# A hybrid decoder layer on one core: low parts of the first weights dealt by hand, and the 64-to-128 step of a block inverse in fours in one PSUM bank

## The chip, the cores and the metric

The kernel runs on one core of a Trainium2 chip. The metric is device time in microseconds of one execution: 1597.19 us before, the median of three runs (1596.48 to 1598.59).

## The reference

One layer over 256 positions of width 2048, in float32. From the vector c come a shift, a scale and a gate (adaLN). Then, in the reference's own words:

```
h = RMSNorm_pre(x) * (1 + scale) + shift
[gdn_qkv | gdn_a | gdn_b | gdn_z | ml_qk | ml_v | ml_i | ml_f | ml_o | ml_z | g_A | g_B] = h W_in
y_A = W_pA( RMSNorm_head(GatedDeltaNet(conv(q, k, v), decay, beta)) * silu(gdn_z) )
y_B = W_pB( sigmoid(ml_o) * RMSNorm_head(mLSTM(conv(q, k), v, i, f)) * silu(ml_z) )
out = (sigmoid(g_A) * y_A + sigmoid(g_B) * y_B) W_out
x <- x + gate * RMSNorm_post(out)
```

The gated delta rule has 32 value heads of 128 on 16 key heads. In it a triangular system `unit_lower @ sol = rhs` is solved per head. The kernel solves it over blocks of 128 positions, so each head needs the inverse of two unit triangular 128 x 128 matrices.

## The kernel before

**The stream.** All large products take 2048-wide weights from memory in units of 1 MB (`load_w`, three buffers). A unit is used in two pieces of 1024 columns. For float32 accuracy each piece is split into a high part `whi` (a rounding copy on ACT, line 169) and a low part `wlo` (a subtraction, line 170, on DVE or on POOL), four buffers each; each product is three matmuls, high x high, high x low and low x high (`mm3`, line 227). `Stream.run` writes the order out: it prepares pieces until more than `ahead` are waiting (1 in the first units, then 3), uses one, calls `after`, and then calls `side.step()`. The kernel is in program order on each engine; no scheduler reorders it.

**The side work.** `Side.step()` advances every generator by one `yield`, lower rank first. So "a step" is one piece of the stream on PE with what the generators issue behind it. Each of PE's small works takes PSUM banks from a ring of four (`gtile`, `banks`, `gfree`): `banks(n)` yields until the next n banks of the ring have been given back in an earlier step. `side.debt` is a reckoning of DVE's load that only decides in which step the base inverse (`base_inverse`) issues its next DVE instructions.

**The beginning.** `first_chunk` (popped from `begin`) is the preparation of the first unit: it issues `keep_busy` matmuls on zeros, the squares of x, the adaLN sums of chunk 0, and chunk 0 of h. x is transposed on PE two chunks at a time (`x_turn`, evicted by ACT, line 338). An adaLN unit `ar` (1 MB, three buffers) is one DVE instruction (line 414) that gives one sum; `h_chunk(k)` needs the two sums of chunk k and makes chunk k of h: `sh`, `s1`, `hf`, then its high and low part. For chunk 1 DVE makes `sh` and `s1` (lines 417 to 420), for the later ones ACT (lines 388 and 389). `BLOCKS` (in `add_start_groups`) say which of the first 14 column groups use which chunks of h, and when the next adaLN unit is put between. Partial sums go to `part` (lines 473, 475, 477).

Which engine makes a low part in this stretch is said by `split_w`: `share[0]` starts at -320 and gains 0.8 of the width at each call; once it is at least the width, POOL takes the piece. When the last adaLN unit is prepared the share becomes 0 and DVE takes all.

**The delta rule.** It runs in eight groups zg of four heads. A period of the stream has 24 pieces: 8 of a q, k, v, v projection (PSUM tile `pt`), 8 of a z projection (`pn`), and 8 of the next `pt`. Each `pt` starts a `gdn_stage1`: convolution (four ACT products at line 651, then DVE at 657), the score matmuls `psa`, `psb` and the transposes `psv` after `yield from banks(3)`, then in the following steps the DVE products that make `au`, and last the right hand sides `rr` (ACT, line 762), four steps behind `psa`. `rr` has two buffers, one group in each.

`base_inverse` makes the inverses of the 32-blocks on DVE. `gdn_stage2` then joins them on PE and applies them: 32-blocks to 64-blocks in two steps (`mp` line 846, `mx` lines 857 and 860), 64-blocks to 128 in two steps (`mq` line 872, evicted to `p2` on ACT, then `mz` line 881, evicted to `x0` on ACT), and then `pa` (893), `pb` (901), `pc` (911) and `po` (919 to 922) with waits of one or two steps between; ACT's line 912 evicts `pc` into `ys`, which line 922 reads. It has rank 0, the first stages rank 1, `base_inverse` rank 2.

Of the kernel before, what the change touches and what calls it, by code (L numbers as in the profile page):

```python
# [9 lines left out]
AF = mybir.ActivationFunctionType  # L10
ALU = mybir.AluOpType
# [4 lines left out]
P = 128  # L16
S = 256
D = 2048
KC = D // P
# [5 lines left out]
START_SHARE = 0.8  # L25
# [92 lines left out]
def hybrid_layer_kernel(  # L118
# [25 lines left out]
    V, A, T, G, SP = nc.vector, nc.scalar, nc.tensor, nc.gpsimd, nc.sync  # L144
# [23 lines left out]
    def split(src, hi, lo, eng=None):  # L168
        A.copy(hi, src)  # L169
        (eng or V).tensor_tensor(lo, src, hi.bitcast(F32), op=ALU.subtract)  # L170

    share = [-320.0, START_SHARE]
    begin = []

    def split_w(src, hi, lo):

        n = src.shape[1]
        share[0] += share[1] * n
        if share[0] >= n:
            share[0] -= n  # L180
            split(src, hi, lo, G)
        else:
            split(src, hi, lo)
# [14 lines left out]
    def gtile(nm, held=False):  # L198
        i = slots[0] % 4
        slots[0] += 1  # L200
        t = pg.tile([P, 512], F32, name=nm, tag="g")
        freed[i] = 1 << 30 if held else side.t + 1
        slots[1][id(t)] = i, t
        return t

    def gfree(t):
        freed[slots[1].pop(id(t))[0]] = side.t

    def banks(n):

        while any(freed[(slots[0] + j) % 4] >= side.t for j in range(n)):
            yield
# [16 lines left out]
    side = Side()  # L229
# [35 lines left out]
    ad = sp.tile([P, 32], F32, name="ad")  # L265
    s1 = sp.tile([P, KC], F32, name="s1")
    sh = sp.tile([P, KC], F32, name="sh")
# [20 lines left out]
    bat = cp.tile([P, 32], F32, name="bat")  # L288
    npre = cp.tile([P, KC], F32, name="npre")
# [8 lines left out]
    zero = part[-1][:, 0]  # L298
    G.memset(zero, 0.0)
    zps = jtile("zps")  # L300

    def keep_busy(n):

        for _ in range(n):
            T.matmul(zps, zero[:, 0:P], zero, start=True, stop=True)

    late_c = {}

# [33 lines left out]
    bnp = sp.tile([P, KC], F32, name="bnp")  # L342
# [6 lines left out]
    def first_chunk(src, hi, lo):  # L349


        keep_busy(4)
        half = [slice(i * 1024, (i + 1) * 1024) for i in range(2)]
        for b in range(2):
            for i in range(2):
                if b == 0 and i == 1:
                    V.scalar_tensor_tensor(part[3].rearrange("p b c -> p (b c)"), xs[:, b, half[i]], 1.0,
                                           xs[:, b, half[i]], op0=ALU.mult, op1=ALU.mult, accum_out=ss[:, b, i:i + 1])
                else:
                    A.activation(part[2].rearrange("p b c -> p (b c)"), xs[:, b, half[i]], AF.Square,  # L360
                                 accum_out=ss[:, b, i:i + 1])
        G.tensor_tensor(rs, ss[:, :, 0], ss[:, :, 1], op=ALU.add)
        G.tensor_scalar(rs, rs, 1.0 / D, EPS, op0=ALU.mult, op1=ALU.add)
        pow_(rs, rs, mhalf[:, 0:2])
        for k in (0, 2, 4, 6, 8):
            x_scale(k)
        ada_sum(ar0, slice(0, D), ad[:, 0:1])
        V.scalar_tensor_tensor(bnp, bat[:, KC:2 * KC], 1.0, npre, op0=ALU.add, op1=ALU.mult)
        for i in range(2):
            ada_sum(ar1, half[i], adh[:, i:i + 1])  # L370
        V.tensor_tensor(ad[:, KC:KC + 1], adh[:, 0:1], adh[:, 1:2], op=ALU.add)
        V.scalar_tensor_tensor(s1[:, 0:1], ad[:, KC:KC + 1], npre[:, 0:1], bnp[:, 0:1], op0=ALU.mult, op1=ALU.add)
        A.activation(sh[:, 0:1], ad[:, 0:1], AF.Identity, bias=bat[:, 0:1])
        V.tensor_copy(hi, src)
        xps = x_turn(0)
        keep_busy(1)
        V.tensor_tensor(lo, src, hi.bitcast(F32), op=ALU.subtract)
        hf = sp.tile([P, S], F32, name="hf", tag="hf", bufs=2)
        A.activation(hf.rearrange("p (b t) -> p b t", b=2), xps[:, :, 0], AF.Identity, bias=sh[:, 0:1],
                     scale=s1[:, 0:1])  # L380
        split(hf, h_hi[:, 0], h_lo[:, 0], V)
        A.copy(xs[:, :, P:2 * P], xps[:, :, 1])
    begin.append(first_chunk)

    def h_chunk(k):

        if k > 1:
            A.activation(sh[:, k:k + 1], ad[:, k:k + 1], AF.Identity, bias=bat[:, k:k + 1])
            A.activation(s1[:, k:k + 1], ad[:, KC + k:KC + k + 1], AF.Identity, bias=bnp[:, k:k + 1],
                         scale=npre[:, k:k + 1])  # L390
        hf = sp.tile([P, S], F32, name="hf", tag="hf", bufs=2)
        A.activation(hf.rearrange("p (b t) -> p b t", b=2), xs[:, :, k * P:(k + 1) * P], AF.Identity, bias=sh[:, k:k + 1], scale=s1[:, k:k + 1])
        split(hf, h_hi[:, k], h_lo[:, k], V if k in (1, KC - 1) else G)
# [14 lines left out]
    def ada_units():  # L408

        adders = []  # L410
        for k in range(1, KC):
            for pt in range(2):
                def prep(h, raw, k=k, pt=pt):
                    V.scalar_tensor_tensor(raw, raw, 1.0, csil, op0=ALU.mult, op1=ALU.mult,
                                           accum_out=ad[:, pt * KC + k:pt * KC + k + 1])
                    if k == 1 and pt:
                        V.scalar_tensor_tensor(s1[:, k:k + 1], ad[:, KC + k:KC + k + 1], npre[:, k:k + 1],
                                               bnp[:, k:k + 1], op0=ALU.mult, op1=ALU.add)
                    elif k == 1:
                        V.tensor_tensor(sh[:, k:k + 1], ad[:, k:k + 1], bat[:, k:k + 1], op=ALU.add)  # L420
                    j = 2 * (2 * k + pt) - 4
                    if 4 <= j < 16:
                        x_turn(j)
                        if 6 <= j < 12:
                            x_scale(j + 4)
                    h_chunks(k - 1)
                    if pt == 1:
                        due.append(k)
                        if k == KC - 1:
                            banks_open()  # L430
                    return ()
                adders.append(lambda i=2 * k + pt, prep=prep:
                              stream.add(w_ada[i], prep, None, 1, load=(load_ada, "ada", ADA_BUFS)))
        return adders
# [22 lines left out]
    def add_start_groups(bi):  # L457
# [41 lines left out]
        for g in groups[::per]:  # L499
            st_ = {}  # L500

            def use_piece(h, hi, lo, g=g, st_=st_):
                for i in range(min(2, per * nk - 2 * h)):
                    gg, c = g + (2 * h + i) // nk, (2 * h + i) % nk
                    if c == 0:
                        st_["ps"] = [jtile(f"pn{i}") for i in range(2)]
                    use(gg, st_["ps"], c, hi, lo, i * 512)
                    if c == nk - 1:
                        after(gg, st_["ps"])
                    if bi == 0 and gg == NE - 2:  # L510
                        h_chunks(1)
                    if bi == 0 and gg == 3:
                        x_turn(2)
                stream.ahead = 3 if bi else 1
            src = tuple(w_in[START[g + i]][:, k0 * 512:(k0 + nk) * 512] for i in range(per))
            adders.append(lambda src=src, use_piece=use_piece:
                          stream.add(src, lambda h, raw: prep_w(h, raw, per * nk * 512), use_piece,
                                     (per * nk + 1) // 2))
# [310 lines left out]
    def gdn_stage2(zg, res, zr):  # L829
# [3 lines left out]
        def um(m):  # L833
            return au[m // 4][:, m % 4 // 2, 256 + 384 * (m % 2):384 + 384 * (m % 2)]
# [28 lines left out]
        for t in range(2):  # L863
            r = 64 * t
            A.activation(x0[r:r + 32, :, r + 32:r + 64], cols32(psx[t])[r:r + 32], AF.Copy, scale=-1.0)
            gfree(psx[t])
        yield
        yield from banks(1)
        psp = gtile("mq", True)
        side.debt -= 1.0  # L870
        for m in range(8):
            T.matmul(psp[64:128, m * 64:(m + 1) * 64], um(m)[0:64, 64:128], y0[:, m], start=True, stop=True)  # L872
        p2 = bp.tile([P, 8, 64], F32, name="p2", tag="p2", bufs=1)
        A.activation(p2[64:128], psp[64:128].rearrange("p (m i) -> p m i", m=8), AF.Copy, scale=-1.0)
        gfree(psp)
        yield
        yield from banks(1)
        psz = gtile("mz", True)
        side.debt -= 1.0
        for m in range(8):  # L880
            T.matmul(psz[0:64, m * 64:(m + 1) * 64], p2[64:128, m], x0[64:128, m, 64:128], start=True, stop=True)  # L881
        A.copy(x0[0:64, :, 64:128], psz[0:64].rearrange("p (m i) -> p m i", m=8))
        gfree(psz)
        yield

        rr = res["rr"].rearrange("p b z (h d) -> p b (z h d)", h=2)
        ys = bp.tile([P, 2, 512], F32, name="ys", tag="ys", bufs=1)
# [587 lines left out]
```

## Time and profile before

| | |
|---|---|
| median of three runs | 1597.19 us |
| profiled execution | 1597.11 us |
| its span | 1595.1 us |
| granted TensorE clock | 0.998 |
| busy share of PE, DVE, ACT, POOL | 99%, 72%, 59%, 16% |

The span is the time between the first and the last instruction of the profiled execution; its own time is 2.0 us longer. PE is the matmul row, and its instructions are pipelined, so a share of 99% says that it hardly ever waits, not that it is at its peak. A row of a timeline gives start, duration, engine, line, operation, output and inputs, and in brackets the idle time ahead of it and what ended it. A row of the chain gives start, duration and what the end of the program was waiting for in that time. A row of the waits gives who waited for whom: total, times, longest.

### The profile page before, as it was taken

The page shows a single profiled execution, that of the slowest core. Times are in us where ns is not written, and L with a number is a line of the kernel's source. Part 1 is how long each engine was busy: PE and PEld are TensorE (multiplying, and loading weights), DVE is VectorE, ACT ScalarE, POOL GpSimd, SP SyncE. Part 2 cuts the span into 40 slices and gives each one's busy share as a digit, 9 for nine tenths or more (in the row PEclk, how much of TensorE's full clock was granted, in tenths as well). Part 3 has the DMA queues.
Part 4 walks back from the last instruction along what each step waited for, and adds up shares of the span by engine and source line. Part 5 has one row for each costly group of instructions (what it writes and reads, how often), then busy time and mean ns, then how long its engine had stood idle before and what let it go on. Part 6 is the DMA issues. An engine that isn't in the chain of part 4 may idle for free.

```text
span 1595.1 us, 25488 instructions
## 1 busy us (share of the span) xinstructions
PE 1581.4 (99%) x9854; PEld 1389.0 (87%) x9854; DVE 1146.5 (72%) x1804; ACT 937.1 (59%) x1494; POOL 250.6 (16%) x206
## 2 busy tenths in 40 slices
PE   8999999999999999999999999999999999999998
PEld 5888888899999999999999999889988878888886
DVE  6776556765689788888878888775768766756654
ACT  7755446765666575757576766665566554444443
POOL 5787761000000010000000000000000000100100
PEclk9999999999999999999999999999999999999999
DMA  9998775965565546555646465546778878766573
GB/s 378 393 387 320 268 295 181 297 234 181 189 190 188 189 156 206 167 182 171 193 159 207 154 195 174 187 165 232 279 268 308 320 275 295 282 248 236 206 274 108
DMA packets 96067, 372.37 MB, mean 233 GB/s; under 512 B 26021, under 2 KB 45877, under 8 KB 58185
## 3 DMA queue, kind: packets, MB, share of 16 engines
q1 hardware_dynamic: 95848, 370.65, 66.4%
q8 instruction: 77, 1.26, 0.3%
q14 instruction: 44, 0.36, 0.1%
q0 software_dynamic: 96, 0.09, 0.0%
q10 hardware_dynamic: 2, 0.01, 0.0%
HBM read 354.40 MB, written 16.31 MB: 232 GB/s over the span
## 4 chain that ended last, share of the span: by engine, by line
PE 84%; issue 12%; DMA 1%; POOL 1%; ACT 0%; DVE 0%; SPq 0%; DVEq 0%; ACTq 0%; POOLq 0%
PE pn L227 37%; PE pt L227 29%; PE py L227 8%; POOL mg L1265 1%; PE psa L227 1%; DMA raw<-in_dram 1%; PE mz L881 1%; PE mq L872 1%; PE csil L297 0%; PE po L922 0%; PE pa L893 0%; PE po L921 0%; PE pc L911 0%; PE po L919 0%; PE pb L901 0%
## 5 line engine op out<-in xcount | busy, mean ns | idle before, releaser
L170 DVE TENSOR_TENSOR wlo<-raw,whi 128x1024 fp32r<-128x1024 f32 x451 | 554.2, 1237 | 264.1 <-ACT whi L169 262.6
L169 ACT CAST whi<-raw 128x1024 fp32r<-128x1024 f32 x516 | 532.2, 1046 | 308.1 <-PE pn L227 154.4
L227 PE MATMUL pt<-h_hi,whi 128*128 128x256 f32 x1280 | 367.8, 287 | 0.0
L227 PE MATMUL pt<-h_hi,wlo 128*128 128x256 f32 x1280 | 362.1, 283 | 0.0
L227 PE MATMUL pt<-h_lo,whi 128*128 128x256 f32 x1280 | 362.0, 283 | 0.0
L227 PE MATMUL pn<-whi,h_hi 128*128 128x512 f32 x896 | 353.0, 394 | 0.3 <-ACT h_hi L169 0.3
L227 PE MATMUL pn<-wlo,h_hi 128*128 128x512 f32 x896 | 349.4, 390 | 1.5 <-POOL wlo L170 1.5
L227 PE MATMUL pn<-whi,h_lo 128*128 128x512 f32 x896 | 349.2, 390 | 0.0
L227 PEld LDWEIGHTS pt<-h_hi,whi 128*128 128x128 f32 x1280 | 245.3, 192 | 1.4
L227 PEld LDWEIGHTS pt<-h_lo,whi 128*128 128x128 f32 x1280 | 245.4, 192 | 0.3
L227 PEld LDWEIGHTS pt<-h_hi,wlo 128*128 128x128 f32 x1280 | 245.2, 192 | 0.0
L227 PEld LDWEIGHTS pn<-wlo,h_hi 128*128 128x128 f32 x896 | 168.4, 188 | 36.6 <-POOL wlo L170 2.7
L227 PEld LDWEIGHTS pn<-whi,h_hi 128*128 128x128 f32 x896 | 168.3, 188 | 35.4 <-ACT h_hi L169 1.1
L227 PEld LDWEIGHTS pn<-whi,h_lo 128*128 128x128 f32 x896 | 168.2, 188 | 35.4
L170 POOL TENSOR_TENSOR wlo<-raw,whi 128x1024 fp32r<-128x1024 f32 (+1 forms) x65 | 150.2, 2321 | 47.8 <-ACT whi L169 47.6
L227 PE MATMUL py<-whi,yhi 128*128 128x512 f32 x384 | 150.7, 392 | 0.0
L227 PE MATMUL py<-whi,ylo 128*128 128x512 f32 x384 | 149.6, 390 | 0.0
L227 PE MATMUL py<-wlo,yhi 128*128 128x512 f32 x384 | 149.5, 389 | 0.0
L473 DVE TENSOR_TENSOR part<-pn,part 128x512 f32<-128x512 f32 x112 | 73.8, 686 | 45.5 <-PE pn L227 45.3
L169 ACT CAST yhi<-ya 128x512 fp32r<-128x512 f32 x48 | 29.9, 622 | 127.8 <-PE py L227 110.9
L657 DVE SCALAR_TENSOR_TENSOR qs<-pt,gcv,qs 128x255 f32<-128x255 f32 (+2 forms) x192 | 92.2, 480 | 4.6
L170 DVE TENSOR_TENSOR ylo<-ya,yhi 128x512 fp32r<-128x512 f32 x48 | 33.2, 691 | 75.4 <-ACT yhi L169 75.4
(269 smaller groups left out, 1810.6 us busy)
## 6 DMA issues: line engine op xcount, KB each, us to landing
raw<-in_dram SPq DMA_DIRECT2D x259, 1024.0 KB
ar<-in_dram SPq DMA_DIRECT2D x31, 1024.0 KB
raw<-in_dram SPq DMA_DIRECT2D x16, 512.0 KB
ya<-o_dr SPq DMA_DIRECT2D x32, 256.0 KB
gate_dr<-part SPq DMA_DIRECT2D x11, 512.0 KB
gb<-rows SPq DMA_DIRECT2D x20, 256.0 KB
raw<-in_dram SPq DMA_DIRECT2D x6, 768.0 KB
ug<-ud SPq DMA_DIRECT2D x32, 128.0 KB
```

The source lines that it names most:

```text
L169: A.copy(hi, src)
L170: (eng or V).tensor_tensor(lo, src, hi.bitcast(F32), op=ALU.subtract)
L227: T.matmul(ps, l, r, start=start and i == 0, stop=stop and i == 2, skip_group_check=True)
L473: V.tensor_tensor(part[g][:, b], ps[b], part[g][:, b], op=ALU.add)
L657: V.scalar_tensor_tensor(dst[:, n, sh:], src[:, 0:S - sh], taps(n, 3 - sh), dst[:, n, sh:], op0=ALU.mult, op1=ALU.add)
L872: T.matmul(psp[64:128, m * 64:(m + 1) * 64], um(m)[0:64, 64:128], y0[:, m], start=True, stop=True)
L881: T.matmul(psz[0:64, m * 64:(m + 1) * 64], p2[64:128, m], x0[64:128, m, 64:128], start=True, stop=True)
L1265: G.tensor_tensor(mcols(b, hf, cg), mcols(b, hf, cg), s_, op=ALU.add)
```

## The change

There are two edits.

*The beginning.* The low parts of the first eight pieces are dealt by a list, `early` (DVE, POOL, POOL, DVE, DVE, POOL, DVE, POOL); behind it the share starts at 0. One of the four `keep_busy` matmuls at the start is 256 columns wide instead of 512. `sh` and `s1` of chunk 1 are made by ACT in `h_chunk`, as for the later chunks. `x_turn(2)` moves from behind the second unit's use to the fourth unit, between the first and the second chunk of its first column group.

*From 64-blocks to 128.* `mq` and `mz` share one bank, `mqz`: `mq` writes partitions 64 to 127, `mz` partitions 0 to 63. The eight matrices go in two fours over three steps: `mq` of the first four; then `mz` of the first four alternating with `mq` of the second four; then `mz` of the second four. Each step evicts its four on ACT. The bank is given back in the third step. The debt is lowered by 0.5 three times instead of by 1.0 twice.

```diff
-    share = [-320.0, START_SHARE]
+    share = [0.0, START_SHARE]
+    early = [V, G, G, V, V, G, V, G]
...
     def split_w(src, hi, lo):
 
         n = src.shape[1]
+        if early:
+            split(src, hi, lo, early.pop(0))
+            return
...
-    def keep_busy(n):
+    def keep_busy(n, cols=512):
 
         for _ in range(n):
-            T.matmul(zps, zero[:, 0:P], zero, start=True, stop=True)
+            T.matmul(zps[:, 0:cols], zero[:, 0:P], zero[:, 0:cols], start=True, stop=True)
...
-        keep_busy(4)
+        keep_busy(3)
+        keep_busy(1, 256)
...
     def h_chunk(k):
 
-        if k > 1:
-            A.activation(sh[:, k:k + 1], ad[:, k:k + 1], AF.Identity, bias=bat[:, k:k + 1])
-            A.activation(s1[:, k:k + 1], ad[:, KC + k:KC + k + 1], AF.Identity, bias=bnp[:, k:k + 1],
-                         scale=npre[:, k:k + 1])
+        A.activation(sh[:, k:k + 1], ad[:, k:k + 1], AF.Identity, bias=bat[:, k:k + 1])
+        A.activation(s1[:, k:k + 1], ad[:, KC + k:KC + k + 1], AF.Identity, bias=bnp[:, k:k + 1],
+                     scale=npre[:, k:k + 1])
...
-                    if k == 1 and pt:
-                        V.scalar_tensor_tensor(s1[:, k:k + 1], ad[:, KC + k:KC + k + 1], npre[:, k:k + 1],
-                                               bnp[:, k:k + 1], op0=ALU.mult, op1=ALU.add)
-                    elif k == 1:
-                        V.tensor_tensor(sh[:, k:k + 1], ad[:, k:k + 1], bat[:, k:k + 1], op=ALU.add)
...
-                    if bi == 0 and gg == 3:
+                    if bi == 1 and gg == NE and c == 0:
                         x_turn(2)
...
         yield from banks(1)
-        psp = gtile("mq", True)
-        side.debt -= 1.0
-        for m in range(8):
-            T.matmul(psp[64:128, m * 64:(m + 1) * 64], um(m)[0:64, 64:128], y0[:, m], start=True, stop=True)
+        psq = psz = gtile("mqz", True)
         p2 = bp.tile([P, 8, 64], F32, name="p2", tag="p2", bufs=1)
-        A.activation(p2[64:128], psp[64:128].rearrange("p (m i) -> p m i", m=8), AF.Copy, scale=-1.0)
-        gfree(psp)
-        yield
-        yield from banks(1)
-        psz = gtile("mz", True)
-        side.debt -= 1.0
-        for m in range(8):
-            T.matmul(psz[0:64, m * 64:(m + 1) * 64], p2[64:128, m], x0[64:128, m, 64:128], start=True, stop=True)
-        A.copy(x0[0:64, :, 64:128], psz[0:64].rearrange("p (m i) -> p m i", m=8))
-        gfree(psz)
-        yield
+        for i in range(3):
+            side.debt -= 0.5
+            first, second = slice(4 * i, 4 * i + 4), slice(4 * i - 4, 4 * i)
+            for m in range(4 * i, 4 * i + 4):
+                if i > 0:
+                    T.matmul(psz[0:64, (m - 4) * 64:(m - 3) * 64], p2[64:128, m - 4], x0[64:128, m - 4, 64:128],
+                             start=True, stop=True)
+                if i < 2:
+                    T.matmul(psq[64:128, m * 64:(m + 1) * 64], um(m)[0:64, 64:128], y0[:, m], start=True, stop=True)
+            if i > 0:
+                A.copy(x0[0:64, second, 64:128], psz[0:64].rearrange("p (m i) -> p m i", m=8)[:, second])
+            if i < 2:
+                A.activation(p2[64:128, first], psq[64:128].rearrange("p (m i) -> p m i", m=8)[:, first], AF.Copy,
+                             scale=-1.0)
+            if i == 2:
+                gfree(psq)
+            yield
```

## The prediction

> **What bounds the kernel now.** I read the page's totals first, then the waits of PE, then the chain that ended last.
>
> ```profile
> span 1595.1 us, 25488 instructions
> PE 1581.4 (99%) x9854; PEld 1389.0 (87%) x9854; DVE 1146.5 (72%) x1804; ACT 937.1 (59%) x1494; POOL 250.6 (16%) x206
> ...
> PE csil L297 <- ACT ar L295: 3.7, 1, 3.7
> PE pn L227 <- POOL wlo L170: 1.5, 2, 0.8
> PE pn L227 <- ACT h_hi L169: 0.3, 1, 0.3
> ```
>
> PE is the bound: apart from the first 3.7 us it waits 1.8 us in all. So an edit counts in two ways only: by what it adds to or takes from PE's own stream, and by making PE wait where now it does not. The whole run took 1597.1 us, 2.0 more than its span; the median shown is 1597.2, so the sum below, made against 1597.1, holds for the median too.
>
> I count in steps: one half block of weights on PE (24 matmuls, some 2.9 us), and behind it the side work that Side.step hands out.
>
> **Part 1, the step from 64-blocks to 128, on PE.** Before, a group has mq (8 small fp32 matmuls, 16 records) in one step and mz in the next; there are 8 groups.
>
> ```profile
> 531.38 1.07 PE mq L872 x16
> 532.45 3.07 PE pt L227 x24
> 535.52 1.07 PE mz L881 x16
> ...
> 542.25 5.75 PE pt L227 x48
> ...
> 523.94 0.69 PE L846 MATMUL mp<-ycmp,au 32*32 32x32 f32 x32
> 527.62 0.21 PE L857 MATMUL mx<-pcm,xcmp 32*32 32x32 f32 x1
> ...
> 528.12 0.20 PE L860 MATMUL mx<-xcmp,pcm 32*32 32x32 f32 x2
> ...
> 531.31 1.14 PE L872 MATMUL mq<-y,au 64*64 64x64 f32 x16
> L872 PE MATMUL mq<-y,au x128: 218/218/267, 531.3 to 1083.4; 64*64 64x64 f32 x128
> ```
>
> An undisturbed half block takes 5.75 / 2 = 2.88 us, the one behind mq 3.07. So mq costs 1.07 + 0.19 = 1.26 us, and mz the same. Records of one tile follow each other every (1.14 - 0.22) / 15 = 0.0615 us, so 16 of them are 0.98 and a fixed 0.28 is for going into and out of the small form. Both together: 2.52.
>
> After the change there are three such visits, of 8, 16 and 8 records. In the middle one mz of the first four (rows 64 to 127, output 0 to 63) alternates with mq of the second four (rows 0 to 63, output 64 to 127). Does PE run such a pair side by side? The trace has two likenesses. mp alternates two tiles of different rows and outputs: (0.69 - 0.20) / 31 = 0.016 us a record, 0.032 a pair. mx has three tiles and shows its 16 triples from 527.62 to 528.12, 0.033 each. Three tiles at the pace of two: they run side by side, and two of mx's three write one bank. Neither shows two row tiles writing one bank, which is what the new form does. I take the overlap: 8 pairs of records at 0.0615, so each visit is 0.49 + 0.28 = 0.77, three are 2.31, and a group saves 0.21: **-1.7 us** over 8 groups. Without overlap the middle visit is 1.26, a group costs 2.80, and the sum is +2.2. These are the two ends.
>
> The Trainium skill, TensorEngine Tiling (Array Packing), section Restrictions and Gotchas, says that different row tiles cannot access one PSUM bank at the same time; by that the middle visit would not overlap and this part would be +2.2 in place of -1.7. The Trainium skill's page PSUM — Partial Sum Buffer, section PSUM bank collisions raise a hardware error, has different quadrants of one bank as free for two engines at once, which speaks for the overlap. No row here decides between them.
>
> ```profile
> L865 ACT ACTIVATE x<-mx x16: 372/374/377, 528.8 to 1080.0; 32x256 f32<-32x256 f32 x16
> ...
> 536.62 0.58 ACT L882 COPY x<-mz 64x512 f32<-64x512 f32 x1 [2.48 <-PE mz L881]
> ```
>
> ACT's two evictions of 512 columns, 0.58 us each, become four of 256, by the mx row 0.37 each. The 0.3 us more lie in ACT's waits for PE, 2.48 us here; without that cover it is 2.6 us over 8 groups.
>
> **Part 2, the same edit on the order of steps.** It yields three times instead of twice, so pa, pb, pc and po of a group all come one step later. The next group's first stage does not move: its psa asks for the next three banks of the ring of four, and although the new bank is held over three steps, those three are the other ones, free since mp and mx. So psa stays in the second of the three steps. Now the wait that matters:
>
> ```profile
> ACT rr L762 <- PE pc L911: 40.0, 6, 6.7
> ...
> 637.27 0.84 ACT L762 ACTIVATE rr<-psv,sk 128x256 f32<-128x256 f32 x2 [6.66 <-PE pc L911]
> 638.00 1.05 ACT L169 CAST whi<-raw 128x1024 fp32r<-128x1024 f32 x1
> 638.93 0.60 ACT L912 COPY ys<-pc 128x512 f32<-128x512 f32 x1
> 639.41 1.59 ACT L651 ACTIVATE qs<-pt,gcv 128x256 f32<-128x256 f32 x4
> 640.84 1.09 ACT L169 CAST whi<-raw 128x1024 fp32r<-128x1024 f32 x1
> ...
> 636.29 0.89 PE pc L911 x8
> 637.18 2.87 PE pt L227 x24
> 640.05 0.22 PE po L919 x2
> ...
> 640.50 0.22 PE po L922 x2
> ...
> 642.73 17.28 PE pt L227 x144
> ```
>
> rr has two buffers, so the rr of group g+2 can be written only when pc of group g has read its own. It stands in ACT's order four steps behind psa, **one step ahead of pc**, and blocks ACT there 6.7 us, six times (groups 0 to 5). Today that is free: PE has its next half blocks split ahead, and behind rr on ACT only one whi stands before the eviction of pc (L912), which ends at 639.53, ahead of the L922 at 640.50 that reads it.
>
> With pc a step later and rr where it was, rr stands two steps ahead. ACT stays blocked until the later pc, some 9.5 us. Behind rr then stand, in ACT's order: whi, the four conv products (L651, which belong to the step that pc has left), another whi, and only then the eviction of pc. From the end of pc on PE, with the rows above: 0.09 to rr's start, 0.73 rr, 0.93 whi, 1.43 conv, 0.94 whi, 0.60 eviction = 4.72 us. PE meanwhile does one half block (2.87) and the first four records of po (0.45) and stands at L922 after 3.32. **PE waits 1.40 us there**, where it waits for nothing now. A restart costs about 0.1 (29.02 to 29.36 below, where 0.23 is usual). 1.5 x 6 = **+9.0 us**.
>
> Bounds: nothing, if the eviction got ahead of conv and the second whi (it would end 2.35 us after pc, before 3.32); and if po as a whole must wait for the eviction, 1.85 + 0.1 each, +11.7. I take 1.5, since the order on ACT is that of the program.
>
> What is late next is DVE, behind the same whi:
>
> ```profile
> 648.46 1.22 DVE L170 TENSOR_TENSOR wlo<-raw,whi 128x1024 fp32r<-128x1024 f32 x1
> ```
>
> This wlo ends at 649.68, 12.5 us behind pc's end. It is for the fourth half block of the 17.28 above, whose third matmul asks for it at 642.73 + 3 x 2.88 + 0.24 = 651.6: a margin of 1.9 us. From pc's end on DVE's work is the same, while PE has one half block less to do before that matmul and waits 1.5: the margin shrinks by 2.88 - 1.5 to some 0.5. So I add nothing; were it gone and as much again, 0.5 a group, +3 in all.
>
> **Part 3, the beginning.**
>
> ```profile
> 29.02 0.50 PE L227 MATMUL pn<-wlo,h_hi 128*128 128x512 f32 x1 [0.81 <-POOL wlo L170]
> 29.36 0.40 PE L227 MATMUL pn<-whi,h_lo 128*128 128x512 f32 x1
> ...
> 36.57 0.50 PE L227 MATMUL pn<-wlo,h_hi 128*128 128x512 f32 x1 [0.70 <-POOL wlo L170]
> ...
> 46.33 0.50 PE L227 MATMUL pn<-whi,h_hi 128*128 128x512 f32 x1
> ...
> 24.97 0.59 ACT L338 COPY xs<-xps 128x512 f32<-128x512 f32 x1
> 25.45 1.06 ACT L169 CAST whi<-raw 128x1024 fp32r<-128x1024 f32 x1
> ...
> 17.39 1.38 DVE L377 TENSOR_TENSOR wlo<-raw,whi 128x1024 fp32r<-128x1024 f32 x1
> ...
> 30.03 0.58 ACT L475 COPY part<-pn 128x512 f32<-128x512 f32 x1
> ...
> 45.69 1.08 ACT L475 COPY part<-pn 128x512 f32<-128x512 f32 x2
> ...
> 50.74 1.27 ACT L475 COPY part<-pn 128x512 f32<-128x512 f32 x2 [0.26 <-PE pn L227]
> ...
> 39.36 0.44 PE xps L335 x4
> 29.08 0.60 ACT L392 ACTIVATE hf<-xs,sh,s 128x256 f32<-128x256 f32 x1 [2.08 <-DVE s L417]
> ```
>
> The shorter keep_busy gains nothing: the first chunk's second matmul stands on DVE's wlo, which ends at 18.77 and does not move. Of the dealt low parts, worked through the old and the new share, only the fifth and the seventh change, POOL to DVE; the third stays with POOL, so the wait at 29.02 stays. Its whi (25.45) moves up by the 0.48 that the eviction of x_turn(2) took ahead of it. The transposes are paid on PE behind that wait instead: until now they lay in the wait for the second low part, and by the 39.36 piece they cost 0.44. s1 and sh of chunk 1 go from DVE to ACT, two instructions of a few tenths of a us that fit into ACT's idle 2.08 ahead of hf; no stall of PE hangs on them. With 0.48 - 0.44, and a bank that DVE's shorter queue frees earlier (PE's 29.36 to 29.64 instead of 0.23, and the like), I make PE 0.2 us earlier at 32, a sum of tenths. The fifth low part on DVE takes the wait of 0.70 away, with its restart about 0.9. But from 30.03 until 50.74 no row of ACT has an idle in front, and at 46.33 PE starts on a bank that ACT's eviction of 45.69 has just left. ACT does the same work in this stretch as before, in the same order, and starts it with the last eviction before 33 us, which waits for PE and is 0.2 us earlier. So PE comes to 46.33 at most 0.2 earlier, and waits there instead: **-0.2 us**. Ends: all 1.5 us of POOL's waits gone, and the transposes and new bank waits paid in full, +0.6.
>
> **Sum.** 1597.1 + 9.0 - 1.7 - 0.2 = **1604.2 us**.
>
> **Rivals.**
> *The two row tiles don't overlap* (the Tiling page's rule, above, gives this). For it: no row shows one bank. Against: mp and mx. With the wait, 1597.1 + 9.0 + 2.2 - 0.2 = 1608.1.
> *The cover holds.* PE doesn't wait at po, because ACT's order has the eviction early enough, or psa and rr slip a step along with pc. Then 1597.1 - 1.7 - 0.2 = 1595.2; with no overlap besides, 1599.1. For it: today's 6.7 us of blocked ACT cost PE nothing, and an eviction 1.4 us earlier decides. Against: the count of the steps.
> *The cover holds and the beginning gives all of its 1.5 us*: 1597.1 - 1.7 - 1.5 = 1593.9. Against: the row at 46.33.
> *DVE's margin goes too*: 1604.2 + 3 = 1607.2.
>
> **Chances.** Forecast 66% (by itself 1600.5 to 1606.5), no overlap with the wait 10%, DVE late too 3%, cover holds 12%, cover holds without overlap 3%, everything gained 6%. Within 0.2% (1594.0 to 1600.4, what a measurement of this kernel can't tell from no change): 15%; slower 79%; faster 6%. The range 1598.5 to 1609.0 leaves out the two cases below 1596, 18%.
>
> **What would show it.** ACT's wait of rr for pc goes from 40.0 to some 57 us, still six times; six waits of PE at po for ys, 1.4 us each; the middle visit of the new bank about as long as the outer two; half blocks behind three visits a group at 3.07. At the beginning one of the two waits for POOL's wlo is gone and a PE wait for ACT's part near 46 us is there. I am wrong if po starts without a wait, or if rr's wait for pc is no longer than 6.7 us.

## The result and the profile after

The changed kernel takes 1639.97 us (median of four, 1638.22 to 1642.12), beside 1597.26 for the kernel before on the same chip: a ratio of 1.0268, with a 95% interval of 1.0255 to 1.0281. It is slower, as forecast, but by 43 us where 7 were forecast.

The first lines of the page of the changed kernel; the profiled execution took 1642.12 us.

```profile
span 1640.3 us, 25503 instructions
PE 1594.8 (97%) x9854; PEld 1390.8 (85%) x9854; DVE 1143.2 (70%) x1804; ACT 938.8 (57%) x1512; POOL 241.7 (15%) x204
```

PE still has its 9854 matmuls, but the span less PE's busy time is 1640.3 - 1594.8 = 45.5 us where it was 1595.1 - 1581.4 = 13.7. So 31.8 of the 45.2 us by which the span grew are idle time of PE. The other 13.4 are busy time, although the change takes a little work away. Part of it is clock (the mean granted clock is 0.993 instead of 0.998; the last section shows a stretch), part the slower start behind each wait (0.50 us for the first matmul instead of 0.39); how much is whose was not separated. By the mean clock alone it would be 8 us (an estimate: 0.007 x 1640 - 0.002 x 1595), but the same estimate gives 21 us for `pb_sooner` further down (clock 0.985), whose PE is busy only 14 us longer, so it is a rough one.

The waits of the changed kernel (engine and line that waits, what it waits for: us in all, times, longest):

```profile
ACT rr L761 <- PE pc L914: 57.2, 6, 9.5
...
ACT dd L689 <- POOL dd L681: 45.0, 12, 6.7
...
PE pn L231 <- ACT whi L169: 13.0, 6, 3.1
...
PE po L925 <- ACT ys L915: 8.9, 6, 1.5
...
PE pn L231 <- DVE wlo L170: 6.7, 10, 1.7
```

The first and the fourth row are the forecast's own (57 and 8.4). The others were not forecast. PE waits 13.0 + 6.7 us in `pn`, the projection of z, for high and low parts; and ACT, which makes the high parts, waits 45.0 us for `dd`, the decay mask. In the kernel before that wait is hardly there:

```profile
ACT dd L690 <- POOL dd L682: 7.3, 4, 2.8
```

What makes `dd` late stands in the chain of work that ended last, here for 646 to 688 us of the changed kernel (start, us, engine, tile and line; "issue" is time without a visible cause):

```profile
646.24 0.91 PE pc L914 x8
...
647.59 0.47 ACT rr L761
648.06 0.94 ACT whi L169
649.02 1.23 DVE wlo L170
650.25 0.75 DVE tmp L799
651.02 0.56 DVE xx L803
...
663.84 0.41 DVE xx L803
...
671.60 6.12 DMA gb<-rows
...
682.49 0.94 ACT whi L169
```

`tmp` and `xx` are the base inverse on DVE; its last piece ends at 664.25, 17.1 us behind the end of `pc`. Then comes a DMA, `gb`, the rows from which `dd` is made. It belongs to the next pair's first stage and needs nothing of the inverse. Why it follows the inverse is seen on SP, the engine that issues it. SP's issues in the kernel before, and then in the changed one:

```profile
648.58 0.38 SPq L809 DMA_DIRECT2D xd<-xx  x1
650.91 3.15 SPq L813 DMA_DIRECT2D xcmp<-xd  x4
654.16 3.64 SPq L164 DMA_DIRECT2D raw<-in_dram  x2
657.89 0.38 SPq L675 DMA_DIRECT2D gb<-rows  x1
```

```profile
618.81 1.50 SPq L674 DMA_DIRECT2D gb<-rows  x1
...
664.28 0.38 SPq L808 DMA_DIRECT2D xd<-xx  x1
668.25 2.77 SPq L812 DMA_DIRECT2D xcmp<-xd  x4
671.12 0.38 SPq L164 DMA_DIRECT2D raw<-in_dram  x1
671.60 0.38 SPq L674 DMA_DIRECT2D gb<-rows  x1
```

SP issues in program order. In the changed kernel `xd` waits for the inverse, `xcmp` reads back what `xd` wrote and is issued 4 us later, and right behind it, without a gap, come the next unit of weights and `gb`. In the kernel before two units of weights stand between `xcmp` and `gb`, and `xd` was early enough. Before, `gb` went out 20.7 us behind `pc`'s end (637.18); now it is 24.5 (647.15). It lands 6.1 us after its issue. By then ACT stands at `dd`, and behind `dd` in ACT's order is the `whi` that PE needs:

```profile
677.85 0.77 POOL L681 TENSOR_SCALAR_AFFINE_SELECT dd<-gb 128x256 f32<-128x256 f32 x2 [10.61 <-DMA gb<-rows]
678.29 0.41 ACT L689 ACTIVATE dd<-dd,ngt 128x128 f32<-128x128 f32 x1 [5.51 <-POOL dd L681]
...
683.48 0.50 PE L231 MATMUL pn<-whi,h_hi 128*128 128x512 f32 x1 [1.91 <-ACT whi L169]
```

So there are two losses in each of six groups: PE's wait at `po`, which was forecast, and this chain, which was not.

### The profile page after: what moved, and what is told of

Read it like the earlier page. It is cut to its first block, busy times and chain, and to the rows that moved or that the text cites. A ratio compares the mean times of both kernels' runs of the same rounds, so it can differ in the third digit from the quotient of the medians.

```text
span 1640.3 us, 25503 instructions
## 1 busy us (share of the span) xinstructions
PE 1594.8 (97%) x9854; PEld 1390.8 (85%) x9854; DVE 1143.2 (70%) x1804; ACT 938.8 (57%) x1512; POOL 241.7 (15%) x204
## 4 chain that ended last, share of the span: by engine, by line
PE 66%; issue 14%; DVE 8%; ACT 6%; DMA 5%; POOL 2%; SPq 0%; DVEq 0%; ACTq 0%; POOLq 0%
PE pn L231 33%; PE pt L231 21%; PE py L231 6%; DVE wlo L170 3%; DMA gb<-rows 3%; ACT whi L169 2%; DMA ya<-o_dr 2%; DVE qs L656 1%; POOL mg L1268 1%; DVE tmp L799 1%; DVE xx L803 1%; ACT qs L650 1%; PE mqz L876 0%; PE pc L914 0%; PE pa L896 0%
## 5 line engine op out<-in xcount | busy, mean ns | idle before, releaser
L231 PE MATMUL pn<-whi,h_hi 128*128 128x512 f32 x896 | 357.2, 399 | 14.0 <-ACT whi L169 13.0
L231 PE MATMUL pn<-wlo,h_hi 128*128 128x512 f32 x896 | 353.2, 394 | 7.5 <-DVE wlo L170 6.7
L231 PEld LDWEIGHTS pn<-whi,h_hi 128*128 128x128 f32 x896 | 169.9, 190 | 52.5 <-ACT whi L169 15.6
L170 POOL TENSOR_TENSOR wlo<-raw,whi 128x1024 fp32r<-128x1024 f32 (+1 forms) x63 | 145.6, 2318 | 50.5 <-ACT whi L169 50.5
L472 DVE TENSOR_TENSOR part<-pn,part 128x512 f32<-128x512 f32 x112 | 73.7, 685 | 45.3 <-PE pn L231 45.2
```

The costliest lines, as they stand in the source:

```text
L231: T.matmul(ps, l, r, start=start and i == 0, stop=stop and i == 2, skip_group_check=True)
L472: V.tensor_tensor(part[g][:, b], ps[b], part[g][:, b], op=ALU.add)
```

## The experiments

Where a time is called a single run, it stands beside a single run of 1597.05 us of the kernel before on the same chip; the others are medians of 4 to 11 runs. Ratios are against the kernel before on the same chip, with a 95% interval. The lateness of `gb` is compared over one period, from the `gb` issue ahead of it to the one behind the inverse (before: 611.61 to 657.89, 46.3 us; after: 618.81 to 671.60, 52.8).

### Which of the two edits

`begin_only` is the kernel before with the edits of the beginning, `inverse_only` the kernel before with the new 64-to-128 step.

> The kernel before with the first edit alone (the beginning). Theory A: -0.2 us by the trace (first projection of the delta rule, counted from the first matmul of csil), within 0.2% by the time; one wait for POOL's wlo gone, a wait for ACT's part in its place. Rival: it gives the 0.9 us of the second wait too, or costs by its new bank waits.

> The kernel before with the second edit alone (the step from 64-blocks to 128 in fours over three steps). Theory A (all of the loss comes from pc standing one step later while rr stays): within 2 us of the whole change, 1637 to 1643, with ACT's wait of rr for pc at 57 us and six waits of PE at po. Rival B (the two edits hurt together, the beginning has a part): clearly under 1635.

The beginning alone: 1596.81 us, ratio 0.9997 (0.9988 to 1.0006), no difference that can be told. The new step alone: 1643.02 us (a single run), with the waits of the changed kernel: `rr` 57.2, `dd` 44.9, `po` 8.9. The whole loss is the second edit's.

### The order of steps, or the fours

`extra_yield` is the kernel before with one empty step between `mz` and `pa`; `mq`, `mz`, their banks and credits stay as they were.

```
         gfree(psz)
         yield
+        yield
```

`debt_old` is the changed kernel with the old credits:

```
-            side.debt -= 0.5
+            side.debt -= (1.0, 1.0, 0.0)[i]
```

> The kernel before with one bare yield more between mz and pa; the matmuls, the evictions and the banks are those of before. Theory A: the step order is the cause, so the loss is all here too: 1638 to 1646 (some 1.2 us above the second edit alone, since PE's small saving is missing), rr's wait 57 us, PE's wait at po 9 us. Rival C (the form in fours, its three visits or the bank held over them, is the cause): within 5 us of before, 1597 to 1602.

> The whole change, but the reckoning of DVE's load is lowered by 1.0, 1.0 and 0 in the three steps in place of 0.5 each. Theory A: unchanged, 1636 to 1644. Rival D (the base inverse is late because the reckoning gives it less room in these steps, and that is the larger part of the loss): under 1625.

The empty step alone gives 1651.39 us: 54 lost, more than the whole change. So a step more ahead of `pa` is enough for the loss, without the fours and without the shared bank. The changed kernel with the old credits gives 1650.98, the same again. Both are single runs, and both lie above what was expected (1638 to 1646, and 1636 to 1644). In both `rr` waits 57.2 and `po` 8.9, as in the changed kernel, but PE waits longer in `pn` for `whi` (21.1 and 20.7 instead of 13.0). So the three credits of 0.5 gain some 11 us in this order of steps: a reckoning that issues no instruction moves the time by more than my whole forecast of 7.

### The place of gb on SP's queue

`gb_pool` is the changed kernel with `gb` issued by POOL; `gb_pool_before` does the same to the kernel before.

```
-        SP.dma_start(gb, rows[row0:row0 + 2].unsqueeze(0).broadcast_to([P, 2, S]))
+        G.dma_start(gb, rows[row0:row0 + 2].unsqueeze(0).broadcast_to([P, 2, S]))
```

> The whole change, but the load of gb (and of the mLSTM's decay rows) is issued by POOL in place of SP. Theory A in two parts: the waits at po (9 us) stay, and the rest, some 34 us, comes by the load of gb standing behind the late base inverse's xd and xcmp on SP's queue, ACT waiting for dd and no whi being made behind it. Then 1605 to 1615 here, ACT's wait of dd for POOL back from 45 us to under 12. Rival E (the rest comes by DVE's and ACT's backlog itself, and the load of gb is only where it shows): above 1625.

> The kernel before with gb's load on POOL's queue and nothing else. There ACT waited 7.3 us for dd in 4 places and PE hardly for it. If gb's place on SP's queue costs only when the base inverse runs late, this is worth nothing: 1596 to 1598, the same as before. If it already costs in the kernel before, up to 1 us is gained. So the gain of 32 us in the changed kernel is the changed step order's loss given back, not a gain of the queue by itself.

`gb_pool` takes 1607.69 us (a single run), 32 less than the changed kernel. Its list of waits has no row of ACT for `dd` on POOL and none of PE for `whi` any more, while ACT's wait at `rr` (57.2, six times) and PE's at `po` (8.9, six times) are unchanged.

In the kernel before, the same move gives 1596.42, ratio 0.9997 (0.9988 to 1.0006): nothing. So it is no gain by itself; it frees `gb` from the late `xd`. The Trainium skill, DMA: Bandwidth & Descriptors, section Issuing engines are not separate DMA queues, says that issuing DMAs from several engines saves only the issuing time on the sequencer, which is usually small. The kernel before agrees (nothing gained). The changed kernel doesn't: what is saved there is the time for which `gb` stands on SP behind `xd` and `xcmp`.

### ACT's block at rr, or the steps of the inverse

What makes `xd` late? Either ACT, blocked longer at `rr`, holds up `whi`, `wlo` and so DVE; or the credits, which moved, let the inverse's pieces out later. `pb_sooner` (changed kernel, `pb` one step behind `pa`) puts `pc` and `po` back into their old steps; `rr_later` (changed kernel) writes the first `rr` of a period two steps later, behind `pc`.

```
 # pb_sooner, between pa and pb
-        yield from wait(2)
+        yield from wait(1)
 # rr_later, ahead of the writing of rr
-        yield
+        yield from wait(1 if z else 3)
```

> The whole change, but pb comes one step behind pa in place of two, so that pb, pc and po stand in the steps where they stood before. Theory A: rr's wait is back to 40 us, no wait at po, dd's wait back to 7; PE saves 0.15 us a group (visits of 0.60 + 0.19 against 1.07 + 0.19) and 0.2 at the beginning: 1594.5 to 1597. Rival C (the form in fours is the cause): still above 1620.

> The whole change, but the first stage of the first pair of a group writes rr two steps later, behind pc in the program's order. pc, po and what follows stay one step late. Theory A: ACT isn't blocked at all, so no wait at po and no late base inverse: 1594 to 1598, rr's wait under 5 us. Rival F (what is one step later in the second stage hurts by itself, by DVE or by the banks): above 1605.

`pb_sooner` was a surprise: 1646.91 us, ratio 1.0316 (1.0302 to 1.0330), worse than the change itself. The wait at `po` is gone and `rr` waits 6.7 us again, as before. But the inverse is later still:

```profile
666.55 0.43 SPq L808 DMA_DIRECT2D xd<-xx  x1
...
674.82 0.38 SPq L674 DMA_DIRECT2D gb<-rows  x1
```

ACT's wait for `dd` rises to 67.4 us and PE's for `whi` to 30.0. DVE's rows show what is late: between the inverse's last `tmp` (at 656.26) and its last `xx` (at 664.60) stand three low parts and three sets of the convolution's instructions, where in the changed kernel (660.72 and 663.84) stands one of each. DVE is not idle there; the reckoning lets the last piece out later. So the block at `rr` can't be the whole cause. `rr_later` has no wait of `rr` and none at `po`, and still takes 1612.43, ratio 1.0094 (1.0081 to 1.0108), with `dd` at 43.5: without the block, a loss of 15 us stays.

### The steps of the inverse alone

`pb_sooner_debt` is `pb_sooner` with the old credits (the line of `debt_old`). `xd_late` is the kernel before with `xd` alone sent two steps later:

```
-        yield from wait(1)
+        yield from wait(3)
         SP.dma_start(xd.rearrange("qq q rg m i -> (q rg m) qq i"), xx)
...
-        yield from wait(5 - 2 * (zg // 7))
+        yield from wait(3 - 2 * (zg // 7))
         side.debt += 1.1
```

> The changed kernel with pc and po in their old steps and the reckoning of the passes as before (1.0, 1.0 and 0 instead of three times 0.5), gb on SP's queue as it was. If the loss comes from where room lets the base inverse's steps run, which the credits of these steps set, the order is then nearly that of before: the last step of the inverse, xd and gb are back within one step of their old places, dd's wait falls from 67 to under 20 us, and the time to 1594 to 1605. If the credits of the passes are not what holds the inverse, it stays at 1635 to 1655, and what holds it is the one step by which pa's credit of 0.8 comes later.

> The kernel before with one thing moved: the base inverse sends xd two steps later (three waits of a step instead of one ahead of it) and takes up xcmp after three steps instead of five, so that everything behind it stands in its old step. No pass, no credit, no PE or ACT order is changed, rr waits as before (6.7 us). If a late xd is itself the cause, by the load of gb that stands behind xd and xcmp on SP's queue, gb is issued some 5 us later, dd's wait on ACT grows to 30 to 45 us and the kernel loses 5 to 20 us (the changed kernel with the later rr, whose gb was issued 2.6 us later than before, lost 15). If the loss needs the changed credits or ACT's block, it stays within 3 us of 1597.

`pb_sooner_debt` takes 1596.07 us, ratio 0.9995 (0.9986 to 1.0004). The three numbers in the credits are worth 51 us here (1646.91 to 1596.07). SP's issues stand where they stood in the kernel before, to 0.1 us:

```profile
648.53 0.38 SPq L808 DMA_DIRECT2D xd<-xx  x1
650.85 2.77 SPq L812 DMA_DIRECT2D xcmp<-xd  x4
657.85 0.38 SPq L674 DMA_DIRECT2D gb<-rows  x1
```

`xd_late` takes 1615.67, ratio 1.0122 (1.0101 to 1.0143), 19 us lost with no change to PE's or ACT's order; `rr` still waits 40.0 us, six times 6.7. `gb` goes out at 664.67 instead of 657.89, and two waits appear that follow from it (dd's is a little below the 30 to 45 expected):

```profile
ACT dd L690 <- POOL dd L682: 27.0, 10, 3.8
...
PE pn L227 <- ACT whi L169: 6.0, 6, 1.7
```

A late `xd` alone is enough. The table puts the runs together; the second column is the number of steps by which the program has `xd` ahead of the next `gb` (counted in the order the program writes, not measured; it is the same in the six groups in which `rr` waits).

| kernel | steps from xd to gb | one wait of rr, us | gb over one period, us | time, us |
|---|---|---|---|---|
| before | 4 | 6.7 | 46.3 | 1597 |
| pb_sooner_debt | 4 | 6.7 | 46.2 | 1596.1 |
| rr_later | 2 | none | 49.1 | 1612.4 |
| xd_late | 2 | 6.7 | 50.2 | 1615.7 |
| extra_yield | 3 | 9.5 | 52.5 | 1651.4 |
| debt_old | 3 | 9.5 | 52.4 | 1651.0 |
| changed | 2 | 9.5 | 52.8 | 1640.0 |
| pb_sooner | 1 | 6.7 | 55.1 | 1646.9 |

Both causes act, and through the same `gb`. Fewer steps between `xd` and `gb` make it late by themselves (`rr_later`, `xd_late`, `pb_sooner`). The later `pa` to `po` take one step of the four (`extra_yield`, `debt_old`), the smaller credits another (the changed kernel beside `debt_old`). ACT's longer block adds to it: with the same two steps the changed kernel's `gb` is 3.7 us later than that of `rr_later`, since DVE starts the inverse's last pieces behind a late `whi` (5.25 us idle ahead of the low part of 649.02).

The time follows `gb` with one exception: `extra_yield` and `debt_old` are 11 us slower than the changed kernel at nearly the same `gb`. ACT's rows of `debt_old` show where it comes from:

```profile
682.86 1.66 ACT L819 COPY x<-xcmp 32x256 f32<-32x256 f32 x4
684.54 3.89 ACT L169 CAST whi<-raw 128x1024 fp32r<-128x1024 f32 x4
```

The inverse is one step earlier in the program's order there, and so the four copies of `xcmp` stand ahead of the first `whi` behind `dd`; in the changed kernel they stand behind it. That `whi` starts at 684.54 instead of 682.36, 1.7 us of it by the copies and 0.5 by the later `dd`. PE waits 20.7 us for `whi` instead of 13.0, and the mean granted clock is 0.990 instead of 0.993.

### Both losses mended

`gb_pool_rr` is `gb_pool` with the edit of `rr_later`; `gb_pool_pb` is `gb_pool` with that of `pb_sooner`.

> The changed kernel with both repairs: the load of gb given to POOL's queue (alone it took 1640 to 1607.7) and rr written two steps later for the first pair of a period (which alone took away ACT's block at rr and the po wait of 8.9, and left 1612.4). If the loss is two separate costs, gb behind xd and xcmp on SP's queue (some 34 us) and ACT's longer block at rr (8.9 us of po wait), both are gone and only the savings of the two edits are left: 1.2 us on the passes and 0.2 in the beginning, so 1594 to 1598. If they are one cost seen twice, or if the later rr only trades ACT's block for DVE's work in the same stretch (PE's waits on DVE's wlo were 6.7 there), it stays at 1600 to 1608.

> The changed kernel with gb on POOL's queue and pb one step behind pa, so that pc and po stand in their old steps. pb one step sooner alone made it worse (1646.9) with no po wait but with 67 us of ACT waiting for dd. If that loss was all gb behind xd and xcmp, it goes with the queue: no po wait, no long dd wait, 1594 to 1598. If the sooner pb costs something of its own (DVE's r2 earlier, PE waiting for ys or for r2), 1600 or more and a wait at pb or pc in the list.

`gb_pool_rr` takes 1596.31 us, ratio 0.9994 (0.9985 to 1.0003). `gb_pool_pb` takes 1595.27, ratio 0.9989 (0.9980 to 0.9997): the one kernel of this study whose interval lies below the kernel before, by 0.5 to 3 us. `pb_sooner`, among the slowest of the table, becomes the best once `gb` stands on another queue.

Four of the kernels make a table of two by two, as the time over the kernel before on the same chip:

| | `gb` issued by SP | `gb` issued by POOL |
|---|---|---|
| `rr` ahead of `pc` | +42.7 (changed) | +10.6 (`gb_pool`, a single run) |
| `rr` behind `pc` | +15.2 (`rr_later`) | -0.7 (`gb_pool_rr`) |

ACT's block without the late `gb` costs 11.3 us, the late `gb` without the block 15.9. Together they cost 43.4, 16 more than the two apart.

## Why the prediction was wrong, point by point

**The block at rr and the wait at po: right, in mechanism and size.** Six waits of 9.5 us, 57.2 in all, for the 57 foreseen. ACT's rows show the order that the prediction counted: `rr`, `whi`, the conv products, `whi`, the eviction.

```profile
647.22 0.84 ACT L761 ACTIVATE rr<-psv,sk 128x256 f32<-128x256 f32 x2 [9.54 <-PE pc L914]
647.95 1.05 ACT L169 CAST whi<-raw 128x1024 fp32r<-128x1024 f32 x1
648.88 1.58 ACT L650 ACTIVATE qs<-pt,gcv 128x256 f32<-128x256 f32 x4
650.32 1.07 ACT L169 CAST whi<-raw 128x1024 fp32r<-128x1024 f32 x1
651.25 0.63 ACT L915 COPY ys<-pc 128x512 f32<-128x512 f32 x1
```

The eviction ends 4.73 us behind `pc` (651.88 - 647.15), where 4.72 was worked out, and PE's wait is 1.48 a group. `gb_pool`, which has this loss and not the other, stands 11.3 us above `gb_pool_rr`, which has neither, where 9.0 were forecast: PE is idle 9.0 us longer and busy 2.2 longer. By this single run a restart costs nearer 0.4 us than the 0.1 taken.

**"What is late next is DVE ... So I add nothing": this step failed.** The low part that it watched did hold its margin: PE waits for nothing between `po` and the projection of z. But the step looked at one instruction of DVE and took it that "from pc's end on DVE's work is the same". It was not. The base inverse runs there, and its pieces are let out by the reckoning of debt, whose credits the change made smaller (0.5 for 1.0) and, for `pa`, `pb`, `pc` and `po`, one step later. The diff shows this, and the prediction gave the credits no line at all. Nor did it follow the inverse on: to `xd`, to SP's queue, to the `gb` that stands there, and over `dd` on ACT to PE. The trace of before had the row from which to see it: ACT already waited 7.3 us for `dd` there, so `gb` had little slack. The forecast had priced what `gb_pool` measures (+10.6). The other 32 us come through `gb`: 16 of them by the late steps alone (`rr_later`; `xd_late` gave 19 for the same two steps), and 16 only when ACT's longer block makes the inverse later still.

**The visits of PE: right, the saving a little too high.** The chain shows them for one group of the changed kernel; the middle visit runs from 623.89 to 624.50.

```profile
620.21 0.60 PE mqz L879 x8
620.82 3.07 PE pt L231 x24
623.89 0.20 PE mqz L876
...
624.50 0.89 PE psa L231 x3
...
629.27 0.60 PE mqz L876 x8
```

```profile
623.92 0.22 PE L876 MATMUL mqz<-x,p 64*64 64x64 f32 x1
623.93 0.22 PE L879 MATMUL mqz<-y,au 64*64 64x64 f32 x1
```

Sixteen records take 0.61 us, no more than the eight of an outer visit, and a record of `mz` (L876) and one of `mq` (L879) start within 0.01 us of each other: the two row tiles run side by side in one bank. The pace of 0.0615 that the prediction took is 0.0613 by its own division, which changes nothing in the sum. With the 0.19 by which the half block behind is longer, a visit costs 0.79 to 0.80 and not 0.77, so a group saves 2.52 - 2.38 = 0.14 and the kernel 1.1 us, not 1.7. The rule that the prediction weighed against this (the Trainium skill, TensorEngine Tiling (Array Packing), section Restrictions and Gotchas: different row tiles can't access one bank at the same time) doesn't hold for these two tiles, which write different quadrants. The rival without overlap falls.

**The beginning: right.** POOL's wait that stood at 36.57 is gone and the one of 29.02 is smaller. A new one has come, of 0.56 at 25.94, where the transposes of `x_turn(2)` had lain, so the list still counts two. And PE waits for ACT's eviction near 46 us instead:

```profile
25.94 0.50 PE L231 MATMUL pn<-wlo,h_hi 128*128 128x512 f32 x1 [0.56 <-POOL wlo L170]
29.30 0.50 PE L231 MATMUL pn<-wlo,h_hi 128*128 128x512 f32 x1 [0.31 <-POOL wlo L170]
...
46.91 0.50 PE L231 MATMUL pn<-whi,h_hi 128*128 128x512 f32 x1 [0.47 <-ACT part L474]
```

From the first matmul on `csil` to the first of `pt` it is 332.75 us in `begin_only` (3.70 to 336.45) and 333.04 before (3.69 to 336.73): 0.3 less, where -0.2 was forecast. The time itself is 0.4 us below the kernel before, inside its interval.

**The rivals.** "The cover holds" was priced at 1595.2; `gb_pool_pb`, in which it does hold, measured 1595.27. That this is so near is in part luck: the visits save 1.1 us and not 1.7, and `gb_pool_rr` and `pb_sooner_debt`, in which PE doesn't wait at `po` either, measured 1596.3 and 1596.1. In the kernel as it was written it didn't. "DVE's margin goes too" named a neighbouring place, at 3 us, and not the chain that counted. No case of the prediction reached past 1609, so its range could not hold the time.

## What to carry to other kernels

When an edit moves work by a step, follow each engine's program order past that point, the queue that issues DMAs included: here a load that needed nothing of the moved work was as late as the DMA that it stood behind. A planner's credit is an edit like any other, even where it issues no instruction: here three numbers decided between 1646.9 and 1596.1 us. A short wait in the trace of before (7.3 us of ACT for `dd`) marks a chain with little slack, and such a chain should be priced for each stretch that the change makes later.

## What the runs showed of the hardware

A wait of PE can cost clock too. One stretch of the changed kernel (us, busy time of PE, PEld, which loads PE's weights, DVE, ACT, POOL, then granted clock, DMA share, GB/s), and rows of PE in it:

```profile
768.00:780.00 12.00, 9.34 (x28) 6.79 (x27) 7.76 (x19) 10.19 (x23) 0.70 (x1) 0.72 0.25 89
```

```profile
772.08 0.80 PE L231 MATMUL pn<-whi,h_hi 128*128 128x512 f32 x1 [2.19 <-ACT whi L169]
773.34 0.79 PE L231 MATMUL pn<-wlo,h_hi 128*128 128x512 f32 x1 [0.46 <-DVE wlo L170]
773.93 0.63 PE L231 MATMUL pn<-whi,h_lo 128*128 128x512 f32 x1
774.36 0.63 PE L231 MATMUL pn<-whi,h_hi 128*128 128x512 f32 x1
...
778.62 0.46 PE L231 MATMUL pn<-wlo,h_hi 128*128 128x512 f32 x1
```

Behind the wait of 2.19 us the matmuls start 0.43 us apart, where 0.23 is usual. The twelve that start from 773.34 up to 778.62 take 5.28 us instead of 2.8, so some 2.5 us are lost on top of the wait. In the group quoted further up, with a wait of 1.91 us, the clock from 680 to 690 us stayed at 1.00. By whole runs the mean clock falls with the longest wait of PE after its first: it is 0.997 to 0.999 in the kernels where none is above 1.7 us, 0.993 at 3.1 (the changed kernel), 0.990 at 4.5 (`debt_old`) and 0.985 at 6.0 (`pb_sooner`). So in this kernel a wait of two microseconds or more may cost more than its own length; the length from which it does was not measured.
